# Expert weights of a mixture-of-experts block: loads of 8 KB per partition in 11 of 19 ring places

## The chip, the cores and the metric

The kernel runs on one core of a Trainium2 chip. The metric is device time in microseconds, from launch to the last result, of one execution; the median of three runs is given. Work is spread over five engines: TensorE (PE, with its weight loads shown as PEld), VectorE (DVE), ScalarE (ACT), GpSimd (POOL) and SyncE (SP, which here only issues DMAs). Data come from HBM through 16 DMA engines.

## The reference, cut to what matters

Two transformer blocks are computed on 256 tokens of width 1024, in float32. The first ends with a routed mixture of experts: each token picks one of 4 groups and 2 of its 8 experts, and each of the 32 experts is a gated product with three weight matrices.

```python
def expert_block(args):            # 32 experts, w1 and w3: 1024 x 512, w2: 512 x 1024
    xb, e = args
    hid = jax.nn.silu(xb @ w1[e]) * (xb @ w3[e])
    return hid @ w2[e]
...
x = x + ga1[:, None, :] * (merged @ w_o[l])          # just ahead of it
h2 = modulate(rms_norm(x, g_norm2[l]), sh2, sc2)
x = x + ga2[:, None, :] * hierarchical_moe(h2, ...)  # then the second block
```

All weights of all 32 experts are read: 32 x 6 MB, some 201 MB of the 333 MB that the kernel moves.

## The kernel before, in words

**Stages.** The first block's dense part (modulation, projections, attention, a short convolution) runs until about 215 us, the product with `w_o` and the router until 250 us, the experts until about 720 us, and the second block until 1146 us. In the dense parts each weight tile of 8 KB per partition (`raw`, 7 buffers) is cut by `split_w` (L169) into a rounded part `hi`, written by ACT (L174), and a rest `lo`, written by DVE (L175), each 4 KB per partition with 4 buffers; `mm3` (L188 to L190) then multiplies three times.

**Experts.** They go in 8 groups of four (`QUAD`). Each expert takes at most 32 tokens, so four experts fill the 128 columns of the array side by side. `moe_up` (L1147 on) walks the 1024 rows of `w1` and then of `w3` in 8 blocks of 128 rows each, `moe_down` (L1199 on) the 512 rows of `w2` in 4 blocks. `gather` (L1070 on) picks and turns the tokens of a group: its matmuls (L1079) load columns of `x1` as weights, every second column (`pair`, L471), because a partition holds two neighbouring rows of the expert weights and the tokens' features must come in the same order. The transposes that feed the router (L874) and the modulation's columns (L509) go by the same order.

**The ring.** `plan_experts` lists 192 items of 1 MB: each is two loads of 512 KB, of two experts, with two neighbouring rows of an expert (4 KB without a break) per partition. `fetch_experts` (L1024 on) issues them on SP's queue in this order, into 19 ring places whose buffers are borrowed from other pools: 4 places of kind `w` (two work tiles), 7 of kind `r` (one `raw` tile), 4 of kind `s` (a `hi` and a `lo` tile), 4 of kind `w`. `expert_tiles` takes two items (four loads, one for each expert) out of the queue for each step of two blocks of rows, and asks for the next items behind them. A load waits on SP until PE has read what its buffer held. The last group's `w2` comes in halves of 512 columns (2 KB pieces), in 8 items, so that the second block can begin while the other half is still multiplied.

**Ahead of the experts.** `moving` (L218 on) multiplies by `w_o`; for the second tile of 128 tokens each half of 512 columns is done in two pieces of 256 neighbouring columns. For each piece `fin` adds the residual (L865, L866), sums squares (L917), turns the result (L874) and copies it on POOL (L880); the last piece ends in the router's chain. `fetch_experts(4)` is called before `w_o`'s product, `fetch_experts(RING)` at the start of `moe`.

Of the kernel before, what the change touches and what calls it, by code (L numbers as in the profile page):

```python
# [17 lines left out]
P = 128  # L18
# [65 lines left out]
class Kernel:  # L84
# [133 lines left out]
    def moving(self, W, c0, xT, nk, consume, split=(), halves=False):  # L218
# [6 lines left out]
        for k0 in range(0, nk, 4):  # L225
# [5 lines left out]
            for i, s in order:  # L231
                t, a, b = pieces[i]
                if last:
                    hi, lo = parts[s // 2]
                elif i == 0:
                    hi, lo = split.pop(0) if v is None else self.split_w(v[:, s:s + 2, :])
                for j in range(2):
                    k = k0 + s + j
                    xh, xl = xT(k)
                    self.mm3(ps[i], (xh[:, t * P:(t + 1) * P], xl[:, t * P:(t + 1) * P]),  # L240
                             (hi[:, j, a:b], lo[:, j, a:b]), k == 0, k == nk - 1)
                if last and s == 2:
                    consume(t, ps[i], *([a] if halves else []))
                if (s == 2) if last else (i == len(pieces) - 1):
                    yield
# [172 lines left out]
    def consts_next(self):  # L418
# [19 lines left out]
        self.vec3 = self.half("vec3")[0:12, 0:256]  # L438
        nc.gpsimd.dma_start(self.vec3[0:8], A["b_ada"][:, 3072:5120].rearrange("a (k d) -> (a k) d", d=256))
        nc.gpsimd.dma_start(self.vec3[8:12], A["g_norm2"].rearrange("a (k d) -> (a k) d", d=256))  # L440
        for w, c0, c1 in (("w_rg", 0, 4), ("w_re", 4, 36)):
            for j in range(2):
                nc.sync.dma_start(self.wrt[:, j::2, c0:c1], A[w][0].rearrange("(a p j) c -> p a j c", a=4, j=2)[:, :, j])
# [7 lines left out]
    def consts_late(self):  # L451
# [5 lines left out]
        for j in range(2):  # L457
            nc.tensor.transpose(ps[:, 12 * j:12 * j + 12], self.vec3[:, j::2], self.c("ident")[:12, :12])
        self.cols["vec3"] = c3 = self.const.tile([P, 24], F32, name="vec3c")
        nc.vector.tensor_copy(c3.rearrange("p (r j) -> p r j", j=2), ps[:, 0:24].rearrange("p (j r) -> p r j", j=2))  # L460
# [42 lines left out]
    def ada_cols(self, j, row, cols):  # L503
# [3 lines left out]
        for m in range(4):  # L507
            d = slice(m * P, (m + 1) * P) if j < 4 else self.pair(m)
            nc.tensor.matmul(ps[:, m:m + 1], row[:, d], self.c("every32"), start=True, stop=True)  # L509
# [257 lines left out]
    def block1(self):  # L767
# [91 lines left out]
        for h in range(2):  # L859
            def fin(t, ps, c0):  # L860
                n = ps.shape[1]
                s = slice(h * 512 + c0, h * 512 + c0 + n)
                x1 = self.x1[t]
                tmp = self.half("res")[:, 0:n]
                nc.vector.tensor_tensor(out=tmp, in0=ps, in1=ga1[:, s], op=OP.mult)  # L865
                nc.vector.tensor_tensor(out=x1[:, s], in0=self.xres[t][:, s], in1=tmp, op=OP.add)  # L866
                self.square_piece(t, x1[:, s])
                last = s.stop == D and t == 1
# [4 lines left out]
                for j in range(0, n, P):  # L873
                    turn = nc.tensor.transpose(ps[:, j:j + P], x1[:, self.pair((s.start + j) // P)], self.c("ident"))  # L874
                to, ps = x1T[t][:, s.start // P:s.stop // P], ps.rearrange("p (j t) -> p j t", t=P)
                if t and s.stop < D:
# [3 lines left out]
                nc.gpsimd.tensor_copy(self.xres[t][:, s], x1[:, s])  # L880
# [4 lines left out]
            self.run_all(self.moving(A["w_o"][0], 512 * h, mT, 8, fin, halves=True))  # L885
# [27 lines left out]
    def square_piece(self, t, x):  # L913

        s = self.small([P, 1], "sqp", 6)
        sq = self.half("sq")[:, 0:x.shape[1]]
# [107 lines left out]
    def fetch_experts(self, n):  # L1024

        while len(self.expert_q) < n and self.expert_next < len(self.expert_order):
# [12 lines left out]
            for v, src in zip(to, parts):  # L1039
                self.nc.sync.dma_start(v if len(src.shape) == 2 else v.rearrange("p (j c) -> p j c", j=src.shape[1]), src)  # L1040
            self.expert_q.append(to)

    def expert_tiles(self):

        v = []
        for _ in range(QUAD // 2):
            v += self.expert_q.pop(0)
# [3 lines left out]
    def plan_experts(self):  # L1051


        A = self.A
        self.expert_q, self.expert_order, self.expert_next = [], [], 0
        self.ahead_of = {}
        for e in range(0, NE, QUAD):
            rows = [(A[n], slice(r, r + 256)) for n in ("w1", "w3") for r in range(0, D, 256)]
            if e + QUAD < NE:
                rows += [(A["w2"], slice(r, r + P)) for r in range(0, 512, P)]  # L1060
            for W, r in rows:
                src = [W[0][e + i, r].rearrange("(p j) c -> p (j c)", p=P) for i in range(QUAD)]
                self.expert_order += [src[i:i + 2] for i in range(0, QUAD, 2)]
        for s in range(2):
            for r in range(0, 512, 256):
                src = [A["w2"][0][NE - QUAD + i, r:r + 256, 512 * s:512 * s + 512].rearrange("(j p) c -> p j c", p=P)
                       for i in range(QUAD)]
                self.expert_order += [src[i:i + 2] for i in range(0, QUAD, 2)]

    def gather(self, E, X):  # L1070
# [76 lines left out]
    def moe_up(self, X, late, steps):  # L1147
# [4 lines left out]
        for m in range(2):  # L1152
# [3 lines left out]
            for k0 in range(0, 8, 2):  # L1156
                next(steps, None)
                v = self.expert_tiles()
                for j in range(2):
                    k = k0 + j  # L1160
                    for i in range(QUAD):
                        s = slice(CAP * i, CAP * i + CAP)
                        nc.tensor.matmul(ps[s], X[:, k, s], v[i][:, j * 512:j * 512 + 512], start=k == 0, stop=k == 7,  # L1163
                                         tile_position=(0, CAP * i))
                if late and m == 0 and k0 == 0:
# [7 lines left out]
    def moe_hidden(self, hid):  # L1173
        nc = self.nc
        ps = self.at()
        for f in range(4):
            nc.tensor.transpose(ps[:, f * P:(f + 1) * P], hid[:, f * P:(f + 1) * P], self.c("ident"))
# [21 lines left out]
    def moe_down(self, hid, ET, ws):  # L1199
        hT = self.moe_hidden(hid)  # L1200
        py = [self.mm() for _ in range(2)]
        for f in range(4):
            v = self.expert_tiles()
            for s in range(2):
                self.moe_product(py[s], hT, f, lambda i: v[i][:, s * 512:s * 512 + 512], f == 0, f == 3)
# [7 lines left out]
    def moe_down_last(self, hid, ET, ws):  # L1213
# [4 lines left out]
        for s in range(2):  # L1218
            for f0 in (0, 2):
                v = self.expert_tiles()  # L1220
                for j in range(2):
                    f = f0 + j
                    self.moe_product(py[s], hT, f, lambda i: v[i][:, j * 512:j * 512 + 512], f == 0, f == 3)
# [34 lines left out]
    def overflow_expert(self, e):  # L1258
# [4 lines left out]
        def piece(W, k, c0, twos):  # L1263
            v = self.half("ov_w")
            if twos:
                src = W[bass.ds(e, 1), k // 2 * 256:k // 2 * 256 + 256, c0:c0 + 512]
                src = src.rearrange("a (p j) c -> p (a j) c", j=2)[:, k % 2]
# [488 lines left out]
```

## Time and profile before

| | before |
|---|---|
| runs, median (lowest to highest) | 1146.39 us (1146.24 to 1149.61) |
| the profiled execution's own time | 1147.72 us |
| its span, first to last instruction | 1146.1 us |
| PE busy, share of the span | 91% |
| DVE, ACT busy | 45%, 33% |
| granted TensorE clock, mean | 0.981 |
| moved by DMA | 332.60 MB, 290 GB/s over the span |

The busy shares are averages over stages with different limits, and a busy PE is no measure of its load, since the ends of matmuls are modelled. How to read the stages: the page cuts the span in 40 slices and gives the busy tenths of each engine, the granted clock, the busy share of the DMA engines and the bytes moved; the chain of work that ended last says, followed back, what each piece of work waited for. A row with a line number names the line of the kernel; `out<-in` are its tiles.

### The profile page before, as it was taken

How to read it: one execution, taken by the hardware profiler on the slowest of the kernel's cores; microseconds unless marked ns; L12 is line 12 of the kernel's file. 1: busy time of each engine (PE TensorE's matmuls, PEld its weight loads, DVE VectorE, ACT ScalarE, POOL GpSimd, SP SyncE). 2: the span in 40 equal slices, each digit the busy share in tenths (PEclk: the TensorE clock that was granted, in tenths of full speed). 3: DMA queues.
4: the chain of work that ended last, by engine and by line, in shares of the span. 5: the costliest groups of instructions: out<-in, count | busy, mean ns of one | idle time of the engine just before them, and what ended most of it. 6: DMA issues, size and time to landing. Idle time of an engine off the chain costs nothing.

```text
span 1146.1 us, 16888 instructions
## 1 busy us (share of the span) xinstructions
PE 1047.4 (91%) x6864; PEld 702.1 (61%) x6866; DVE 515.4 (45%) x882; ACT 383.5 (33%) x618; POOL 47.8 (4%) x60
## 2 busy tenths in 40 slices
PE   5999999989978888888888888999899999999998
PEld 2787699964231313131212213977889899999987
DVE  3776565651130211212121203797577765555555
ACT  3443444521010100000000003766547564444454
POOL 1030000000000000000000000222110000000000
PEclk9999999989989999999999999999999999999999
DMA  9798887889999999999999999955333655555521
GB/s 343 272 365 281 300 280 265 289 324 407 409 409 408 409 408 409 409 409 408 409 410 409 409 404 375 316 159 155 118 102 121 212 190 184 184 184 184 166 74 37
DMA packets 148035, 332.60 MB, mean 290 GB/s; under 512 B 11717, under 2 KB 61729, under 8 KB 147953
## 3 DMA queue, kind: packets, MB, share of 16 engines
q1 hardware_dynamic: 146624, 328.95, 78.2%
q0 software_dynamic: 688, 1.38, 0.4%
q8 instruction: 55, 0.90, 0.3%
q10 hardware_dynamic: 640, 1.14, 0.3%
q14 instruction: 28, 0.22, 0.0%
HBM read 330.38 MB, written 1.05 MB: 289 GB/s over the span
## 4 chain that ended last, share of the span: by engine, by line
PE 54%; DMA 38%; DVE 5%; ACT 2%; issue 1%; SPq 0%; DVEq 0%; ACTq 0%
DMA ew<-w 15%; DMA raw<-w 14%; PE mm L188 13%; PE mm L189 13%; PE mm L190 13%; DMA lo<-w 7%; PE pa L496 2%; DVE lo L175 1%; PE pa L623 1%; DMA raw<-w_ada 1%; PE pb L189 1%; PE pa L189 1%; PE pb L190 1%; PE pa L190 1%; PE pa L188 1%
## 5 line engine op out<-in xcount | busy, mean ns | idle before, releaser
L175 DVE TENSOR_TENSOR lo<-raw,hi 128x1024 fp32r<-128x1024 f32 x192 | 235.3, 1229 | 124.8 <-ACT hi L174 124.1
L174 ACT ACTIVATE hi<-raw 128x1024 fp32r<-128x1024 f32 x192 | 201.8, 1058 | 180.3 <-PE mm L189 109.0
L1163 PE MATMUL mm<-ew,moeX 128*32 128x512 f32 x432 | 112.7, 602 | 14.6 <-DMA ew<-w 14.6
L188 PE MATMUL mm<-hTh,hi 128*128 128x256 f32 x416 | 120.8, 290 | 0.0
L190 PE MATMUL mm<-hTh,lo 128*128 128x256 f32 x416 | 119.3, 287 | 0.0
L189 PE MATMUL mm<-hTl,hi 128*128 128x256 f32 x416 | 118.8, 286 | 0.0
L1170 DVE TENSOR_TENSOR hid<-hid,mm 128x512 f32<-128x512 f32 x8 | 5.5, 687 | 225.3 <-PE mm L1163 225.3
L1163 PE MATMUL mm<-raw,moeX 128*32 128x512 f32 x376 | 92.0, 610 | 11.8 <-DMA raw<-w 10.5
L189 PE MATMUL mm<-fTl,hi 128*128 128x256 f32 x352 | 99.7, 283 | 0.0
L188 PE MATMUL mm<-fTh,hi 128*128 128x256 f32 x352 | 99.6, 283 | 0.0
L190 PE MATMUL mm<-fTh,lo 128*128 128x256 f32 x352 | 99.6, 283 | 0.0
L188 PEld LDWEIGHTS mm<-hTh,hi 128*128 128x128 f32 x416 | 80.1, 192 | 5.6 <-issue 2.4
L190 PEld LDWEIGHTS mm<-hTh,lo 128*128 128x128 f32 x416 | 80.1, 193 | 1.8 <-issue 1.4
L189 PEld LDWEIGHTS mm<-hTl,hi 128*128 128x128 f32 x416 | 80.1, 193 | 1.2 <-issue 1.0
L1163 PEld LDWEIGHTS mm<-ew,moeX 128*32 128x32 f32 x432 | 20.2, 108 | 96.3 <-DMA ew<-w 77.6
L188 PEld LDWEIGHTS mm<-fTh,hi 128*128 128x128 f32 x352 | 67.5, 192 | 0.5
L189 PEld LDWEIGHTS mm<-fTl,hi 128*128 128x128 f32 x352 | 67.5, 192 | 0.4
L190 PEld LDWEIGHTS mm<-fTh,lo 128*128 128x128 f32 x352 | 67.5, 192 | 0.0
L1163 PEld LDWEIGHTS mm<-raw,moeX 128*32 128x32 f32 x376 | 17.0, 109 | 77.1 <-DMA raw<-w 56.9
L1195 DVE SCALAR_TENSOR_TENSOR y<-mm,moews,ga 128x512 f32<-128x512 f32 x16 | 12.0, 748 | 92.9 <-PE mm L1186 92.9
L1140 ACT ACTIVATE moeET<-pb 128x256 fp32r<-128x256 f32 x8 | 3.1, 383 | 148.1 <-PE pb L1138 148.1
L188 PE MATMUL mm<-hi,hTh 128*128 128x512 f32 x128 | 51.9, 407 | 0.0
(405 smaller groups left out, 1843.3 us busy)
## 6 DMA issues: line engine op xcount, KB each, us to landing
ew<-w SPq DMA_DIRECT2D x164, 512.0 KB, 10.2
raw<-w SPq DMA_DIRECT2D x140, 512.0 KB, 10.2
raw<-w_in SPq DMA_DIRECT2D x42, 1024.0 KB, 9.5
raw<-w_ada SPq DMA_DIRECT2D x24, 1024.0 KB, 11.7
hi<-w SPq DMA_DIRECT2D x40, 512.0 KB, 10.2
lo<-w SPq DMA_DIRECT2D x40, 512.0 KB, 10.2
raw<-w_ffn_gate SPq DMA_DIRECT2D x11, 1024.0 KB, 5.3
raw<-w_ffn_up SPq DMA_DIRECT2D x11, 1024.0 KB, 5.4
```

What stands on the lines that cost most here:

```text
L174: nc.scalar.activation(out=hi, in_=v, func=AF.Copy)
L175: nc.vector.tensor_tensor(out=lo, in0=v, in1=hi.bitcast(F32), op=OP.subtract)
L188: nc.tensor.matmul(out, lh, rh, start=first, stop=False, **kw)
L189: nc.tensor.matmul(out, lh, rl, start=False, stop=False, **kw)
L190: nc.tensor.matmul(out, ll, rh, start=False, stop=last, **kw)
L496: nc.tensor.matmul(ps[32 * g:32 * g + 32], self.cb[:, 4 * half + g, :], v[half][:, g, :], start=half == 0, stop=half == 1, tile_position=( ...
L623: nc.tensor.matmul(o, qz[h // 4][:, h % 4, t * P:(t + 1) * P], key(h)[:, 0:L], start=True, stop=True)
L1140: nc.scalar.activation(out=ET, in_=ps[:, 0:T], func=AF.Copy)
L1163: nc.tensor.matmul(ps[s], X[:, k, s], v[i][:, j * 512:j * 512 + 512], start=k == 0, stop=k == 7, tile_position=(0, CAP * i))
L1170: nc.vector.tensor_tensor(out=hid, in0=hid, in1=up[1], op=OP.mult)
L1195: self.nc.vector.scalar_tensor_tensor(out=y, in0=ps, scalar=ws, in1=self.ga2[:, sl], op0=OP.mult, op1=OP.mult)
```

## The change

An item of the ring becomes four neighbouring rows of one expert (8 KB without a break per partition, 1 MB in all) instead of two rows of two experts. In places of kind `r` and `s` (11 of 19) it is one load of 1 MB; in places of kind `w`, whose two work tiles are separate, it stays two loads with 4 KB per partition each, the front and the back half of each 8 KB piece. For that, `hi` and `lo` of `split_w` become the two halves of one tile of 8 KB per partition (tag `spl`, 4 buffers). A step takes four items instead of two and works on four blocks of rows. Two places of the order stay fine (two items a step, two experts an item): the first four items of all, and the last four of `w3` in the last group; the last group's `w2` stays in 2 KB pieces. The features now come in fours: `gather`, the transposes for the router and the modulation's columns read every fourth column, and for the second tile of tokens `moving` takes, as a piece of 256 columns, two neighbours of every four instead of 256 neighbours, so that `fin` works on such columns too. The router's weights and some vectors are loaded in the same order.

```diff
 def split_w(self, v):
-        hi = self.spl_p.tile([P, a, b], F32R, tag="hi", name="hi")
-        lo = self.spl_p.tile([P, a, b], F32R, tag="lo", name="lo")
+        both = self.spl_p.tile([P, 2, 1024], F32R, tag="spl", name="hilo")
+        hi, lo = (both[:, i, 0:a * b].rearrange("p (a b) -> p a b", a=a) for i in range(2))
...
 def moving(...):
+                    o, w = ps[i], [x[:, j, a:b] for x in (hi, lo)]
+                    if fours and t:
+                        o, w = o.rearrange("p (g f) -> p g f", f=2), [self.fours(x[:, j], a // 128) for x in (hi, lo)]
...
-    def pair(k):
-        o = 256 * (k // 2) + k % 2
-        return slice(o, o + 255, 2)
+    def every(n, k):
+        o = n * P * (k // n) + k % n
+        return slice(o, o + n * (P - 1) + 1, n)
+    def fours(a, c):
+        return a.rearrange("p (g f) -> p g f", f=4)[:, :, c:c + 2]
...
 def fetch_experts(self, n):
-            if kind == "r":
-                r = self.raw()
-                to = [r[:, 0:1024], r[:, 1024:2048]]
-            elif kind == "s":
-                to = [self.spl_p.tile([P, 1024], F32, tag=tag, name=tag) for tag in ("hi", "lo")]
+            if kind == "w":
+                to = [self.work("ew") for _ in range(2)]
             else:
-                to = [self.work("ew") for _ in range(2)]
+                t = self.raw() if kind == "r" else self.spl_p.tile([P, 2048], F32, tag="spl", name="es")
+                to = [t[:, 0:1024], t[:, 1024:2048]]
+            if len(parts) == 1 and kind != "w":
+                self.nc.sync.dma_start(t, parts[0])
+            else:
+                if len(parts) == 1:
+                    parts = [parts[0][:, 0:1024], parts[0][:, 1024:2048]]
...
 def plan_experts(self):
-            rows = [(A[n], slice(r, r + 256)) for n in ("w1", "w3") for r in range(0, D, 256)]
+            rows = [(A[n], slice(r, r + 512)) for n in ("w1", "w3") for r in range(0, D, 512)]
...
-                self.expert_order += [src[i:i + 2] for i in range(0, QUAD, 2)]
+                if (e, n) in ((0, 0), (NE - QUAD, 3)):
+                    for h in range(2):
+                        half = [a[:, 1024 * h:1024 * h + 1024] for a in src]
+                        self.expert_order += [half[i:i + 2] for i in range(0, QUAD, 2)]
+                        self.expert_fine.append(True)
+                else:
+                    self.expert_order += [[a] for a in src]
+                    self.expert_fine.append(False)
...
 def gather(self, E, X):
-                    nc.tensor.matmul(o[j], self.x1[t][:, self.pair(k0 + j)], E[:, t], start=t == 0, stop=t == 1)
+                    nc.tensor.matmul(o[j], self.x1[t][:, self.every(4, k0 + j)], E[:, t], start=t == 0, stop=t == 1)
```

## Rows read from the trace of the kernel before

**Rows 1.** Page, part 4: the chain that ended last, shares by engine.
```profile
PE 54%; DMA 38%; DVE 5%; ACT 2%; issue 1%; SPq 0%; DVEq 0%; ACTq 0%
```

**Rows 2.** The chain in order of time: start us, us, what.
```profile
254.13 1.85 PE mm L1163 x16
...
262.37 10.29 DMA raw<-w
...
683.96 10.79 DMA ew<-w
694.79 1.92 PE mm L1186 x10
```

**Rows 3.** Windows: length, busy us of engines (count), clock, DMA share, GB/s.
```profile
149.00:156.00 7.00, 7.00 (x61) 7.00 (x60) 2.92 (x4) 2.18 (x3) 0.00 (x0) 1.00 1.10 348
686.00:704.00 18.00, 13.54 (x62) 5.12 (x64) 7.08 (x14) 6.41 (x13) 0.00 (x0) 0.91 1.05 387
300.00:650.00 350.00, 295.51 (x1382) 88.57 (x1379) 54.43 (x120) 26.74 (x53) 0.00 (x0) 0.97 1.03 409
```

**Rows 4.** DMA view of the same three windows, in that order: packets by size.
```profile
DMA packets 2405, 2.44 MB, mean 348 GB/s; under 512 B 39, under 2 KB 2389, under 8 KB 2405
...
DMA packets 3594, 6.96 MB, mean 387 GB/s; under 512 B 195, under 2 KB 195, under 8 KB 3594
...
DMA packets 39253, 143.15 MB, mean 409 GB/s; under 512 B 4355, under 2 KB 4355, under 8 KB 39233
```

**Rows 5.** Page, part 6: loads into raw by SP, KB each, us to landing.
```profile
raw<-w SPq DMA_DIRECT2D x140, 512.0 KB, 10.2
```

**Rows 6.** SP's queue, waits: two rows of 262:700 us, then one of 246:262.
```profile
SPq L1040 <- DMA ew<-w: 120.8, 133, 2.4
...
SPq L1040 <- PE mm L1163: 2.3, 6, 1.0
...
SPq L1040 <- PE mm L1163: 10.9, 3, 8.6
```

**Rows 7.** Timeline of SP's queue, 254.5:264 us: start, us, loads issued.
```profile
255.99 4.98 SPq L1040 DMA_DIRECT2D ew<-w  x8
```

**Rows 8.** Windows at the experts' start, and three of 10 us inside.
```profile
254.00:258.00 4.00, 4.00 (x38) 1.79 (x40) 0.82 (x2) 0.85 (x2) 0.00 (x0) 1.00 0.45 145
...
310.00:320.00 10.00, 7.14 (x31) 2.98 (x29) 2.15 (x7) 0.38 (x1) 0.00 (x0) 0.93 1.03 411
340.00:350.00 10.00, 6.88 (x27) 1.76 (x31) 1.87 (x4) 0.00 (x0) 0.00 (x0) 0.54 1.03 408
350.00:360.00 10.00, 9.15 (x54) 1.91 (x50) 0.00 (x0) 0.60 (x1) 0.00 (x0) 1.00 1.02 407
```

**Rows 9.** One line's instructions, L874 and L313: duration ns min/median/max.
```profile
L874 PEld LDWEIGHTS pb<-cst,x x16: 194/209/221, 225.8 to 243.4; 128*128 128x128 f32 x16
...
L313 PEld LDWEIGHTS pb<-cst,xres x48: 138/140/230, 700.2 to 1120.7; 128*128 128x128 f32 x48
```

**Rows 10.** The chain again: runs of matmuls with such weights.
```profile
255.98 1.14 PE pb L1079 x8
...
716.31 0.96 PE pb L313 x7
```

**Rows 11.** Timeline of PE in the product with w_o: two neighbouring matmuls.
```profile
224.38 0.28 PE L190 MATMUL mm<-hi,ml 128*128 128x256 f32 x1
224.50 0.28 PE L188 MATMUL mm<-hi,mh 128*128 128x256 f32 x1
```

**Rows 12.** Groups by line and shape, 224:262 us: DVE and ACT on one piece.
```profile
L866 DVE TENSOR_TENSOR x<-xres,res 128x256 f32<-128x256 f32 x4 | 1.9, 468 | 0.1
...
L917 ACT ACTIVATE sq<-x 128x256 f32<-128x256 f32 x4 | 1.7, 415 | 2.7 <-DVE x L866 2.7
```

**Rows 13.** Page, part 5: the split's first half on ACT.
```profile
L174 ACT ACTIVATE hi<-raw 128x1024 fp32r<-128x1024 f32 x192 | 201.8, 1058 | 180.3 <-PE mm L189 109.0
```

**Rows 14.** Page, part 3: the queue with the largest packets.
```profile
q8 instruction: 55, 0.90, 0.3%
```

More of the change, by code (lines that the diff above doesn't have):

```diff
@@ L216, in stat_unit, with moving @@
             yield
-    def moving(self, W, c0, xT, nk, consume, split=(), halves=False):
+    def moving(self, W, c0, xT, nk, consume, split=(), halves=False, fours=False):
         split = list(split)
@@ L437, in consts_next @@
             ("norm_ffn_g_2", 8), ("norm_ple_g_2", 8))], nc.gpsimd)
-        self.vec3 = self.half("vec3")[0:12, 0:256]
-        nc.gpsimd.dma_start(self.vec3[0:8], A["b_ada"][:, 3072:5120].rearrange("a (k d) -> (a k) d", d=256))
-        nc.gpsimd.dma_start(self.vec3[8:12], A["g_norm2"].rearrange("a (k d) -> (a k) d", d=256))
+        self.vec3 = self.half("vec3")[0:6]
+        nc.gpsimd.dma_start(self.vec3[0:4], A["b_ada"][:, 3072:5120].rearrange("a (k d) -> (a k) d", d=512))
+        nc.gpsimd.dma_start(self.vec3[4:6], A["g_norm2"].rearrange("a (k d) -> (a k) d", d=512))
         for w, c0, c1 in (("w_rg", 0, 4), ("w_re", 4, 36)):
-            for j in range(2):
-                nc.sync.dma_start(self.wrt[:, j::2, c0:c1], A[w][0].rearrange("(a p j) c -> p a j c", a=4, j=2)[:, :, j])
+            for a in range(2):
+                nc.sync.dma_start(self.wrt[:, 4 * a:4 * a + 4, c0:c1],
+                                  A[w][0][512 * a:512 * a + 512].rearrange("(p j) c -> p j c", j=4))
         spread(self.brt[:, 0:4], "b_rg", 4)
@@ L860, in fin @@
             def fin(t, ps, c0):
-                n = ps.shape[1]
-                s = slice(h * 512 + c0, h * 512 + c0 + n)
+                n, k0 = ps.shape[1], 4 * h + c0
+                cut = (lambda a: self.fours(a, c0)) if t else (lambda a: a)
+                part = lambda a: cut(a[:, h * 512:h * 512 + 512])
+                flat = (lambda a: a.rearrange("p (g f) -> p g f", f=2)) if t else (lambda a: a)
                 x1 = self.x1[t]
[L864 to L868, printed above, removed]
+                tmp = flat(self.half("res")[:, 0:n])
+                nc.vector.tensor_tensor(out=tmp, in0=flat(ps), in1=part(ga1), op=OP.mult)
+                nc.vector.tensor_tensor(out=part(x1), in0=part(self.xres[t]), in1=tmp, op=OP.add)
+                self.square_piece(t, part(x1), flat)
+                last = k0 == 6
                 if last:
@@ L873, in fin @@
                 for j in range(0, n, P):
-                    turn = nc.tensor.transpose(ps[:, j:j + P], x1[:, self.pair((s.start + j) // P)], self.c("ident"))
-                to, ps = x1T[t][:, s.start // P:s.stop // P], ps.rearrange("p (j t) -> p j t", t=P)
-                if t and s.stop < D:
+                    turn = nc.tensor.transpose(ps[:, j:j + P], x1[:, self.every(4, k0 + j // P)], self.c("ident"))
+                to, ps = x1T[t][:, k0:k0 + n // P], ps.rearrange("p (j t) -> p j t", t=P)
+                if t and not last:
                     nc.scalar.activation(out=to, in_=ps, func=AF.Copy)
@@ L884, in fin @@
                     self.router(1, mean, self.router_logits(x1T[1], range(6, 8), logits, turn))
-            self.run_all(self.moving(A["w_o"][0], 512 * h, mT, 8, fin, halves=True))
+            self.run_all(self.moving(A["w_o"][0], 512 * h, mT, 8, fin, halves=True, fours=True))
         for t in range(2):
@@ L1155, in moe_up @@
                 next(steps, None)
[L1156 to L1165, printed above, removed]
+            v = []
+            for k in range(8):
+                if k % 2 == 0:
+                    next(steps, None)
+                if not v:
+                    v = self.expert_tiles()
+                for i in range(QUAD):
+                    s = slice(CAP * i, CAP * i + CAP)
+                    nc.tensor.matmul(ps[s], X[:, k, s], v[i].pop(0), start=k == 0, stop=k == 7,
+                                     tile_position=(0, CAP * i))
+                v = v if v[0] else None
+                if late and m == 0 and k == 1:
                     late()
@@ L1176, in moe_hidden @@
         for f in range(4):
-            nc.tensor.transpose(ps[:, f * P:(f + 1) * P], hid[:, f * P:(f + 1) * P], self.c("ident"))
+            nc.tensor.transpose(ps[:, f * P:(f + 1) * P], hid[:, self.every(2, f)], self.c("ident"))
         hT = self.half("hidT")
```

55 lines of the change are left out of this document (31 added, 24 removed).

## The prediction, made before the changed kernel was run

> **What bounds the kernel now.** I read the chain of work that ended last first. By engine it is 54% PE and 38% DMA [rows 1], which sounds like a mixture; followed in time it is two stages with one bound each. Up to 254 us and from 695 us on it runs through PE, DVE and ACT; from 262 to 695 us it is nothing but expert loads, one landing after the other, each piece some 10 us long [rows 2]. So 432 us are bound by the DMA engines, and what PE does there costs nothing as long as it keeps up. The windows say how close that stretch is to a limit: 409 GB/s at a DMA share of 1.03 over 350 us [rows 3]. Nothing is idle there, so only the engines' own rate can shorten it. The waits of SP's queue agree: in this stretch it waits for earlier loads (120.8 us for one kind alone), and hardly for PE to give a buffer back (2.3 us) [rows 6]. A load lands 10.2 us after its issue [rows 5], which at 409 GB/s is eight loads of 512 KB, so only 4 of the ring's 19 MB are under way at a time, and the ring has slack.
>
> **What a packet costs.** Three stretches with a DMA share over 1, each with one packet size, tell what the size is worth [rows 3, 4]. Without the small packets below 512 B, 149 to 156 us has 1 KB packets, 686 to 704 us has 2 KB (6.96 MB over 3,399) and 300 to 650 us has 4 KB (143 MB over some 34,900). The time of one packet on one of 16 engines is 16 times its size over the rate: 16 x 1024 / 348 = 47.1 ns, 16 x 2048 / 387 = 84.7 ns, 16 x 4096 / 409 = 160.2 ns. The steps are 37.6 ns for the first KB added and 75.5 ns for the next two (37.8 each): a straight line, 37.7 ns per KB and some 9.4 ns per packet whatever its size. The share of completion packets (one behind eight of 4 KB) is inside the 160.2, and stays one behind eight in a 1 MB load with 8 KB packets.
>
> **The gain.** On that line an 8 KB packet takes 160.2 + 2 x 75.5 = 311.2 ns, two of 4 KB take 320.4. A 1 MB item is 8 such packets on each engine, so it saves 8 x 9.2 = 74 ns of 2.56 us, 2.9%. The number of such items in the DMA-bound stretch comes from the plan. Of 192 items, 0 to 3 and 180 to 191 stay fine. The first 19 are issued ahead of the experts, where SP is held by others; item 19 is the first that waits for PE's first step (issued at 255.99 us [rows 7]). From 19 to 179, places 4 to 14 of the ring occur 8 x 11 = 88 times in the full rounds (items 19 to 170), and 5 times in the last (175 to 179): 93. Gain: 93 x 0.074 = 6.8 us. Ends of the unknown: nothing, if the hardware cuts an 8 KB piece back into 4 KB packets; and, if a packet cost nothing beyond its bytes, 93 x 8 x 18.8 ns = 14.0 us. Between them I take the line, which three points support; rounding of the rates moves it by 0.3 us.
>
> The items in places of kind w stay 4 KB packets, but from rows 8 KB apart. The 2 KB packets of 686 to 704 us are halves of 4 KB rows, too, and lie on the line, so 0. Twice the bytes per load doubles what eight loads hold in flight to at most 8 MB, still within the ring, 0. Some hundred issues on SP fall away; it was waiting anyway.
>
> The Trainium skill has a figure that speaks against this size of gain. On the page "DMA: Bandwidth & Descriptors", section "Why small descriptors are slow (HBM only)", it gives a fixed overhead of some 3 cycles per packet; 32 bytes go in a cycle, so 4 KB takes 131 cycles and 8 KB 259 instead of 262, 1.1%, and the sum would be 2.7 us instead of 6.8. The trace disagrees: its 9.4 ns are 5.9% of a 4 KB packet.
>
> **PE in the experts' stretch.** A step now waits for four items instead of two and then does four blocks of rows. Two blocks take 1.85 us at full clock (the 16 instructions of [rows 2]), four 3.7 us, while four items take some 10.1 us to land. PE works in bursts now, and the clock may fall: before, 340 to 350 us was granted 0.54, nearly the lower level of 1.2 GHz, in a stretch with idle times of PE, and 350 to 360 us, where PE worked on with hardly a gap, 1.00 [rows 8]. At 1.2 GHz throughout, the four blocks take 7.4 us, still under 10.1; and a PE that falls behind works without gaps, which is when the full clock is granted. The remaining slack is the ring, 15 items or some 37 us behind the group in use. Cost 0; if that cover were gone the wait would show on SP for PE. The end of the stretch keeps its fine steps, so what follows the last landing is unchanged.
>
> **The start of the stretch.** Here PE's path counts in full: the DMA engines run dry (share 0.45 from 254 to 258 us [rows 8]), because SP waited up to 8.6 us for PE's first step [rows 6]. The first four items stay fine, so the first eight loads are issued as before, 10.3 us of work from 255.99 us [rows 2, 7]. The third and fourth step become one, so the first `raw` buffer comes back some 2 us later, near 264 us; the queue then still holds some 2 us. Cost 0.
>
> **What lies on PE's path ahead of it.** (a) Weight loads that read every fourth column: 32 for the modulation's columns, 16 transposes (L874), 32 of the first `gather`, 80 in all. No row has this step. Every second column instead of neighbours made the load itself 209 ns instead of 140 [rows 9], while the matmuls with such weights still follow each other by 1.14/8 = 0.143 us against 0.96/7 = 0.137 [rows 10]: hidden behind the matmul. Bounds 0 and 80 x 0.069 = 5.5 us; I take 0.5, nearer the row of the spacing. (b) 96 matmuls of `w_o` (2 pieces, 8 blocks, 3 products, 2 halves) whose moving operand is two neighbours of every four. They follow each other by 0.12 us [rows 11]. No row has such an operand; bounds 0 and a doubling, 96 x 0.12 = 11.5 us. I take 0. (c) DVE and ACT on such columns: on the last piece two of DVE (0.47 us) and one of ACT (0.42) lie on the path [rows 12]; bounds 0 and a doubling, 1.3 us; I take 0.3. POOL's copy has the whole first group to finish. (d) `hi` and `lo` in one tile: ACT now waits for the last of the three products instead of the second, 0.12 us later [rows 13, 11], with three further buffers filled; 0.
>
> On (a) and (b) the Trainium skill, page "SBUF — State Buffer", in its note on cachelines under the port swizzle, says that two accesses in each 16-byte line run at full bandwidth and fewer pay. By it (b) is free and (a) pays; that the load with every second column, which has two, took 209 ns instead of 140 is not what that rule says, and the sum keeps the bounds of rows.
>
> **The sum.** -6.8 + 0.5 + 0.3 = -6.0 us. The profiled execution took 1147.72 us (span 1146.1, so 1.6 around it), 1.3 above the median of the three runs; 1147.72 - 6.0 = 1141.7, and against the median 1146.39 it is 1140.4. What comes next behind the faster stream is still the stream.
>
> **The rivals.** First, 8 KB pieces travel as 4 KB packets: no gain, and the 0.8 us of the start remain, 1147.2. For it speaks that no packet of SP's loads here is above 4 KB, since none was asked for; against it, that the instruction queue has 55 packets of 16 KB [rows 14], so the engines take larger ones. The skill's page on DMA, section "SWDGE vs HWDGE vs iDMA", prefers packets of at most 4096 B, which would make this the outcome; no run shows whether it holds for SP's queue.
> Second, the per-packet cost is smaller than the line's: a gain of 2.7, 1144.5 with the costs; the line speaks against.
> Third, on the other side: pairs out of four as moving operand run at half rate in the product with `w_o`. All of its 11.5 us lie ahead of PE's first step, where SP waits for PE, so they come in full: 1140.4 + 11.5 = 1151.9. It decides once (b) passes 6 us, a slowdown by half. For it speaks (a)'s 209 against 140 ns; against it, that spacing did not follow.
> Fourth, 8 KB packets run slower than two of 4 KB. The 16 KB packets took 0.3% x 16 x 1146 / 55 = 1.0 us each [rows 14], where four of 4 KB take 0.64; but they come one by one, to another place, with their latency inside. Even a tenth of that excess, (1.0 - 0.64) / 2 x 0.1 = 18 ns for 8 KB, would be 93 x 8 x 18 ns = 13 us and 1159.
>
> **How the numbers follow.** The line 0.64, no gain 0.16, the small gain 0.06, half-rate `w_o` 0.10, slow 8 KB packets 0.04. The forecast is the likeliest, 1140.4. Its own range: costs at most some 2.6 us above what I took (1143.0), and a gain a third of the way from 6.8 to 14.0 with no cost (1146.4 - 9.2 = 1137.2). To leave out no more than 2 in 10 the range reaches over the small gain and no gain, to 1148. A measurement of this kernel tells a change of 0.3%, 3.4 us, from none: below 1142.95 is faster. That is the forecast's 0.64, less 0.02 for its upper tail, 0.62; the same is 0.02 + 0.16 + 0.06 = 0.24; slower 0.14.
>
> **What would show it.** Right: over the middle of the experts' stretch some 416 GB/s instead of 409 (11/19 of the bytes 2.9% faster), packets of 8 KB in the DMA view and some 29% fewer packets of data for the same bytes (half as many for 11/19 of them); the last expert load landing some 6 us earlier; the stretch from 695 us on moved as a block. Wrong in the gain: 409 GB/s and no packet of 8 KB. Wrong at the start: PE's first expert step later than 254.1 us, with L188 to L190 of the w_o product further apart than 0.12 us, or L1079 further than 0.143. Wrong on PE: SP waiting for PE inside the stretch for more than a few us, or DMA shares below 1 there.

## The result, and the profile after

| | before | after |
|---|---|---|
| median of 6 runs (lowest to highest) | 1147.30 us (1146.24 to 1149.61) | 1154.62 us (1152.60 to 1155.78) |
| the profiled execution's own time, its span | 1147.72, 1146.1 us | 1154.68, 1153.1 us |

The ratio of after to before is 1.0058 (95% interval 1.0046 to 1.0070): the changed kernel is slower by 7.3 us, where 6 us less was forecast, and lies 6.6 us above the end of the range.

The chain of work that ended last (start us, us, what) divides it into three, as [rows 2] did before:

```profile
270.86 2.65 PE mm L1192 x16
...
695.63 10.77 DMA ew<-w
706.45 1.92 PE mm L1216 x10
```

| stage | before | after | difference |
|---|---|---|---|
| up to the first expert step | 254.13 us | 270.86 us | +16.7 |
| from there to the last landing | 440.7 us | 435.6 us | -5.1 |
| from there to the end of the span | 451.3 us | 446.7 us | -4.6 |

**The stream** did what was forecast. The window of its middle (columns as in [rows 3]) and the DMA view of it answer to [rows 3, 4]:

```profile
300.00:650.00 350.00, 260.94 (x1453) 105.22 (x1454) 57.35 (x126) 27.36 (x54) 0.00 (x0) 0.88 1.02 416
```
```profile
DMA packets 28073, 145.58 MB, mean 416 GB/s; under 512 B 3116, under 2 KB 3116, under 8 KB 17516
```

The rate is 416 GB/s instead of 409. Without the small packets there are 24,957 packets where there were 34,898, which is 28% fewer, and 10,557 of them (28,073 less 17,516) are of 8 KB or more. The granted clock fell from 0.97 to 0.88, at a DMA share that stayed above 1.

**The start** did not. First, two neighbouring matmuls of the product with `w_o` (timeline of PE; start us, duration), for [rows 11]:

```profile
223.83 0.41 PE L188 MATMUL mm<-hilo,mh 128*128 128x256 f32 x1
224.06 0.41 PE L189 MATMUL mm<-hilo,mh 128*128 128x256 f32 x1
```

They are 0.23 us apart instead of 0.12. Second, the chain's runs of matmuls whose weights are every fourth column: a set of modulation columns (L517; the chain of before has L509 x8 with 0.83 us), and a run of `gather` behind the first step, for the 1.14 us of [rows 10]:

```profile
116.38 1.75 PE pb L517 x8
...
273.51 2.06 PE pb L1107 x8
```

The instructions of these lines (duration ns min/median/max) say that the load of weights is what grew, but not for the transposes:

```profile
L1107 PEld LDWEIGHTS pa<-moeEr,x x8: 330/330/330, 268.6 to 270.2; 128*128 128x128 f32 x8
```
```profile
L884 PEld LDWEIGHTS pb<-cst,x x16: 196/206/261, 235.8 to 259.6; 128*128 128x128 f32 x16
```

In `gather` a load takes 330 ns (197 at the median for those into `pa` before), in the transposes 206, as in [rows 9] with every second column. Third, two stretches at half the clock (1.2 GHz of 2.4), each beginning within a microsecond of the end of a set of modulation columns; before was granted 1.00 from 100 to 150 us throughout:

```profile
119.00:122.00 3.00, 3.00 (x12) 2.27 (x12) 0.80 (x3) 1.95 (x3) 0.00 (x0) 0.50 0.49 184
...
137.00:139.00 2.00, 2.00 (x11) 1.88 (x10) 0.86 (x2) 0.67 (x2) 0.00 (x0) 0.50 1.02 353
```

### The profile page after: what moved, and what is told of

Read it like the earlier page. It is cut to its first block, busy times and chain, and to the rows that moved or that the text cites. A ratio compares the mean times of both kernels' runs of the same rounds, so it can differ in the third digit from the quotient of the medians.

```text
span 1153.1 us, 16719 instructions
## 1 busy us (share of the span) xinstructions
PE 1018.3 (88%) x6866; PEld 732.6 (64%) x6868; DVE 515.3 (45%) x882; ACT 383.4 (33%) x618; POOL 48.2 (4%) x60
## 3 DMA queue, kind: packets, MB, share of 16 engines
q10 hardware_dynamic: 640, 1.14, 0.3%
## 4 chain that ended last, share of the span: by engine, by line
PE 59%; DMA 33%; DVE 5%; ACT 2%; issue 1%; SPq 0%; DVEq 0%; ACTq 0%
DMA ew<-w 16%; PE mm L188 13%; PE mm L190 13%; PE mm L189 13%; DMA raw<-w 10%; DMA es<-w 6%; PE pa L504 2%; PE mm L1216 2%; PE mm L1192 2%; PE pa L631 1%; PE pb L1107 1%; DVE hilo L175 1%; PE pa L1107 1%; DMA raw<-w_ada 1%; PE pb L517 1%
## 5 line engine op out<-in xcount | busy, mean ns | idle before, releaser
L175 DVE TENSOR_TENSOR hilo<-raw,hilo 128x1024 fp32r<-128x1024 f32 x192 | 235.3, 1229 | 131.9 <-ACT hilo L174 131.5
L174 ACT ACTIVATE hilo<-raw 128x1024 fp32r<-128x1024 f32 x192 | 201.8, 1057 | 165.1 <-PE mm L190 107.5
L188 PE MATMUL mm<-hTh,hilo 128*128 128x256 f32 x416 | 120.6, 290 | 0.0
L190 PE MATMUL mm<-hTh,hilo 128*128 128x256 f32 x416 | 119.2, 287 | 0.0
L189 PE MATMUL mm<-hTl,hilo 128*128 128x256 f32 x416 | 118.6, 285 | 0.0
L189 PE MATMUL mm<-fTl,hilo 128*128 128x256 f32 x352 | 99.6, 283 | 0.0
L190 PE MATMUL mm<-fTh,hilo 128*128 128x256 f32 x352 | 99.5, 283 | 0.0
L188 PE MATMUL mm<-fTh,hilo 128*128 128x256 f32 x352 | 99.5, 283 | 0.0
L188 PEld LDWEIGHTS mm<-hTh,hilo 128*128 128x128 f32 x416 | 80.1, 193 | 5.8 <-issue 2.5
L190 PEld LDWEIGHTS mm<-hTh,hilo 128*128 128x128 f32 x416 | 80.1, 193 | 1.9 <-issue 1.5
L189 PEld LDWEIGHTS mm<-hTl,hilo 128*128 128x128 f32 x416 | 80.1, 193 | 1.2 <-issue 1.0
L188 PEld LDWEIGHTS mm<-fTh,hilo 128*128 128x128 f32 x352 | 67.4, 192 | 0.5
L190 PEld LDWEIGHTS mm<-fTh,hilo 128*128 128x128 f32 x352 | 67.5, 192 | 0.0
L188 PE MATMUL mm<-hilo,hTh 128*128 128x512 f32 x128 | 51.5, 404 | 0.0
L189 PE MATMUL mm<-hilo,hTh 128*128 128x512 f32 x128 | 50.7, 396 | 1.0 <-DVE hilo L175 1.0
```

Source lines behind the costliest of these rows:

```text
L188: nc.tensor.matmul(out, lh, rh, start=first, stop=False, **kw)
L189: nc.tensor.matmul(out, lh, rl, start=False, stop=False, **kw)
L190: nc.tensor.matmul(out, ll, rh, start=False, stop=last, **kw)
```

## The experiments

The theory after the result: PE's strided reads ahead of the first step cost the 16.7 us (S). The rival: PE in bursts, at the lower clock of 0.88, costs it, by the coarse steps (B). All times below are medians, with the ratio to the kernel before. That kernel's median was 1147.30 us beside the changed kernel and 1147.73 to 1147.99 us beside the others, so differences between kernels are good to some 0.7 us. The times in a chain come from one execution of each kernel.

### The strided reads, one at a time

**The moving operand alone.** The halves of `w_o` are written by ACT and DVE in another order of columns, so that PE reads 256 neighbours; for the first tile of tokens DVE's multiplication puts the columns back. All else is the changed kernel.

```diff
+    def split_w4(self, v):
+        src = v.rearrange("p j c -> p (j c)").rearrange("p (m c f) -> p c m f", c=2, f=2)
+        hi, lo = (both[:, i].rearrange("p (c m f) -> p c m f", c=2, f=2) for i in range(2))
...
-                        o, w = o.rearrange("p (g f) -> p g f", f=2), [self.fours(x[:, j], a // 128) for x in (hi, lo)]
+                        w = [x[:, a // 256, j] for x in (hi, lo)]
...
```

> The changed kernel with one part undone: in the product with w_o the split writes hi and lo already in the order in which the pieces need them, so that PE reads 256 neighbouring columns again (it read two of every four). Theory S (PE reads such pairs at half rate, and all of that lies ahead of the experts): the matmuls of the second tile of tokens follow each other by 0.12 us instead of 0.23, 96 x 0.11 = 10.6 us come back, 1144 us, first expert step near 260 us instead of 270.9. Theory B (the loss comes from PE working in bursts of four blocks, with its clock at 0.88 in the experts' stretch instead of 0.97): nothing comes back, 1154 us.

Measured: 1143.57 us, ratio 0.9962 (0.9950 to 0.9974), 11.05 less than the changed kernel. In its chain the first expert step begins 11.65 us earlier:

```profile
259.21 2.93 PE mm L1211 x16
```

**The weight loads alone.** The modulation rows and the tokens are stored in fours, by the copies and additions that write them anyway, so that PE loads 128 neighbours, in the router's transposes too.

```diff
-        nc.vector.tensor_copy(row, ps)
+            nc.vector.tensor_copy(row.rearrange("p (f g) -> p f g", f=4), ps.rearrange("p (g f) -> p f g", f=4))
...
-                nc.vector.tensor_tensor(out=part(x1), in0=part(self.xres[t]), in1=tmp, op=OP.add)
+                nc.vector.tensor_tensor(out=x1n, in0=nat(part(self.xres[t])), in1=nat(tmp), op=OP.add)
...
-                    nc.tensor.matmul(o[j], self.x1[t][:, self.every(4, k0 + j)], E[:, t], start=t == 0, stop=t == 1)
+                    nc.tensor.matmul(o[j], self.x1[t][:, (k0 + j) * P:(k0 + j + 1) * P], E[:, t], start=t == 0, stop=t == 1)
```

> The changed kernel with the other strided reads undone: the modulation's rows and x1 are stored with their features already in fours, so that the weight loads of the modulation's columns, of the router's transposes and of gather read neighbouring columns; the pairs in the product with w_o stay. Theory S: eight loads of columns take 0.83 us again instead of 1.75, four times 0.92 = 3.7 us, the first gather gives some 2 us back and the half clock near 120 us goes (1.7): 7 us in all, 1147.5 us, eight of gather's matmuls in 1.14 us instead of 1.87 to 2.06. Theory B: within 1 us of 1154.6.

Measured: 1148.78 us, ratio 1.0011 (1.0001 to 1.0020), 5.84 less than the changed kernel. A set of modulation columns takes 0.79 us, there is no stretch at half the clock from 100 to 150 us, and the first step comes 6.58 us earlier:

```profile
115.97 0.79 PE pb L520 x8
...
264.28 2.53 PE mm L1197 x16
```

**Both.**

> Both of the above together: 8 KB packets and coarse steps as in the changed kernel, but PE reads no strided columns. Theory S: 1154.6 - 10.6 - 7 = 1137, that is some 9 to 10 us below the kernel before (6.8 of packets, the rest what differs in the second block), first expert step near 254 us, 416 GB/s in the experts' stretch with PE's clock still below 0.95 there. Theory B: no better than the kernel before, 1147 or more.

Measured: 1139.97 us (1138.60 to 1141.25), ratio 0.9929 (0.9916 to 0.9943), 14.65 less than the changed kernel and faster than the kernel before. The clock in the middle of the stream is still 0.89, so B is out as the cause of the loss. But the two parts don't add up: alone they moved the first step by 11.65 and 6.58 us, together by 13.95 (to 256.91), 4.3 less than the sum. The groups by line show one reason: the repair costs DVE something, which PE's slow product had hidden. The addition on 256 columns, 426 ns in the changed kernel, takes 1004 ns in the mean when it writes in fours (two of the four 1.3 to 1.4 us, two 0.6 us):

```profile
L900 DVE TENSOR_TENSOR x<-xres,res 128x256 f32<-128x256 f32 x4 | 4.0, 1004 | 0.1
```

**Both, with POOL turning the tokens.** The addition goes back to the natural order, and the copy that POOL makes in any case writes the tokens in fours; the router's transposes read every fourth column again.

```diff
-                nc.gpsimd.tensor_copy(part(self.xres[t]), part(x1))
+                nc.gpsimd.tensor_copy(x1f, fine(part(x1)))
```

> The kernel with both reads made contiguous (1139.97 us), with one difference: the residual is added in place in the natural order of columns, the router's transposes read every fourth column again, and POOL's copy, not DVE's addition, writes the tokens in fours for the gather. If the price of the repair lies in DVE's addition (its row grew from 426 to 1004 ns for 256 columns, and 1.3 us of it stand in the chain behind each of the two last pieces), the first expert step begins 1.3 to 2.6 us earlier than 256.9, and the time is 1137.4 to 1138.7 us. If the two repairs overlap for another reason, or if the gather now waits for POOL's copy, the first step stays at 256.9 or comes later and the time is 1140 or more.

Measured: 1139.31 us (1138.11 to 1139.66), ratio 0.9924 (0.9910 to 0.9938). The first step comes 2.46 us earlier than the 256.91 of the version above, and is again where the kernel before had it (254.13):

```profile
254.45 2.71 PE mm L1216 x16
...
679.24 10.78 DMA ew<-w
690.06 1.92 PE mm L1240 x10
```

The medians are only 0.7 us apart, less than expected, and the runs of the two overlap: the worth of this last step in the whole time is not settled.

With it the start adds up, if each chain is cut at the first of the four sets of columns that the change strides and at the first matmul of the product with `w_o` (start in us, then the length of the two parts):

| kernel | first set | `w_o` | first expert step | set to `w_o` | `w_o` to step |
|---|---|---|---|---|---|
| before | 104.76 | 215.76 | 254.13 | 111.00 | 38.37 |
| no strided reads, POOL turning | 104.50 | 215.34 | 254.45 | 110.84 | 39.11 |
| no strided reads, DVE turning | 105.51 | 216.35 | 256.91 | 110.84 | 40.56 |
| strided loads alone | 105.50 | 220.22 | 259.21 | 114.72 | 38.99 |
| strided `w_o` alone | 104.45 | 215.30 | 264.28 | 110.85 | 48.98 |
| the changed kernel | 103.89 | 221.77 | 270.86 | 117.88 | 49.09 |

The strided `w_o` costs 9.9 us (39.11 to 48.98), the strided loads 3.9 (110.84 to 114.72), the turning on DVE 1.45 (39.11 to 40.56), which is within what was expected; the other 1.0 us of the 2.46 lie ahead of `w_o`, where these two versions are the same program. The changed kernel has another 3.2 us ahead of `w_o` (114.72 to 117.88), and its two stretches at half the clock lie there. The version with strided loads alone runs the same program up to `w_o` and has none, so they vary from one execution to the next. Of the kernels whose columns are loaded with every fourth, two of three profiled executions have one or two such stretches; of the eight others none has. What sets them off is not shown. Both repairs came out without them, so that these 3.2 us were counted twice; with the 1.7 that DVE's turning took back from the gain behind `w_o`, and 0.5 the other way ahead of the first set, that is the 4.3.

### The operand by itself

32 matmuls of each kind, each with 128 x 128 weights, behind the kernel before; the added work lengthens the span to 1232.9 us. The granted clock is 1.00 in all of it.

```diff
+        for _ in range(n):
+            nc.tensor.matmul(o, w, m[:, 256:512], start=True, stop=True)
+        for _ in range(n):
+            nc.tensor.matmul(o, w, m[:, 0:512:2], start=True, stop=True)
+        for _ in range(n):
+            nc.tensor.matmul(two(o, 2), w, four[:, :, 0:2], start=True, stop=True)
+        for _ in range(n):
+            nc.tensor.matmul(two(o, 4), w, eight[:, :, 0:4], start=True, stop=True)
...
+            nc.tensor.matmul(q, f[:, 0:256:2], f[:, 512:640], start=True, stop=True)
...
```

> The kernel before with blocks of 32 equal matmuls behind its end, to measure PE's reads by themselves: float32r matmuls of 256 columns whose moving operand is contiguous, every second, two of four, four of eight, eight of sixteen, every fourth; then float32 matmuls of 128 columns whose weights are contiguous, every second, every fourth, every eighth column. Theory S by 16-byte pieces: the cost follows how much of each 16 bytes is used: contiguous, four of eight and eight of sixteen 0.12 us each, every second and two of four 0.23, every fourth 0.23 or more; weights 0.14 us per matmul for contiguous and every second column, 0.25 for every fourth. Rival (any step costs the same): four of eight and eight of sixteen at 0.23 too, and weights in every second column slower than contiguous.

The chain of its end, moving operands of 256 columns in the split type first (contiguous; every second; two of every four; four of eight; eight of sixteen; every fourth), then float32 weights (contiguous; every second; every fourth; every eighth), where a matmul is two instructions:

```profile
1153.59 3.84 PE mm L1753 x32
1157.42 7.25 PE mm L1755 x32
1164.68 7.25 PE mm L1757 x32
1171.93 3.77 PE mm L1759 x32
1175.70 3.84 PE mm L1761 x32
1179.54 7.46 PE mm L1763 x32
1187.00 7.15 PE mm L1766 x64
1194.15 7.54 PE mm L1768 x64
1201.69 14.93 PE mm L1770 x64
1216.62 15.22 PE mm L1772 x64
```

Per instruction: a moving operand costs 0.120 us contiguous, 0.227 with two of every four, and 0.118 with four of every eight. Weights cost 0.112 contiguous, 0.118 with every second column and 0.233 with every fourth. So both new reads of the change are of the kind that halves PE's rate, and the read that the kernel before had, every second column as weights, is not.

### The packets

**The changed kernel, every item in two loads of 4 KB per partition.** Strides, tiles and steps stay.

```diff
-            if len(parts) == 1 and kind != "w":
+            if False:
```

> The changed kernel with every expert item in two loads of 4 KB per partition (front and back half of the 8 KB piece), order and steps unchanged: the packet size alone undone. Theory of the packet's fixed cost (9.4 ns): the stretch goes back to 409 GB/s and 93 x 0.074 = 6.8 us are added, 1161 us. Rival (the stream did not gain by packet size but by the order of rows or fewer issues): 416 GB/s and 1154.6 us stay.

Measured: 1160.55 us, ratio 1.0105 (1.0089 to 1.0120), 5.9 us more than the changed kernel. The middle of the stream is back at the rate of [rows 3], at the clock of after:

```profile
300.00:650.00 350.00, 258.49 (x1440) 102.10 (x1441) 56.71 (x124) 26.35 (x53) 0.00 (x0) 0.88 1.03 409
```

**The same without the strided reads.**

> The version without strided reads, with every expert item in two loads of 4 KB per partition: coarse steps and the order in fours remain, 8 KB packets do not. Packet theory: 1140.0 + 93 x 0.074 = 1146.9, 409 GB/s. What then remains against the kernel before is what the coarse steps, the start and the second block cost or give together, near 0 to -1. Rival (coarse steps with their low clock cost several us that the packets hide): 1149 or more.

Measured: 1146.15 us, ratio 0.9991 (0.9982 to 1.0000), 6.2 us more than with 8 KB pieces (1139.97). The chains say the same of the stage alone: from the first step to the last landing 441.7 us in 4 KB pieces (first two lines), 435.4 in 8 KB pieces (last two), 6.3 less.

```profile
255.59 1.85 PE mm L1216 x16
...
697.26 1.92 PE mm L1240 x10
```
```profile
256.91 2.49 PE mm L1216 x16
...
692.30 1.92 PE mm L1240 x10
```

**More places of one load.** The contiguous kernel, with the 8 places of kind `w` used in the first round only.

```diff
-            kind = RING_KINDS[self.expert_next % RING]
+            i = self.expert_next
+            kind = RING_KINDS[i] if i < RING else RING_KINDS[4 + (i - RING) % (RAW + SPL)]
```

> The version without strided reads, with the places of two work tiles used in the first round of the ring only; from item 19 on all items go to the 11 places that take 8 KB without a break. Packet theory: items 19 to 179 are all 8 KB, 161 instead of 93, 68 x 0.074 = 5.0 us less, 1135, 422 GB/s in the stretch. Rival (a ring of 11 MB is too short for PE's bursts and pauses at the end of a group): SP waits for PE inside the stretch, DMA share under 1, 1140 or more.

Measured: 1142.74 us, ratio 0.9955 (0.9941 to 0.9970), 2.8 us more than with the 19 places, although the stream runs faster. Two windows, the DMA view of the second, and SP's waits in 270:680 us:

```profile
260.00:264.00 4.00, 4.00 (x38) 2.02 (x40) 0.83 (x3) 0.46 (x1) 0.00 (x0) 1.00 0.00 0
...
300.00:650.00 350.00, 248.98 (x1416) 85.28 (x1412) 54.42 (x120) 27.34 (x54) 0.00 (x0) 0.90 1.01 421
```
```profile
DMA packets 20223, 147.37 MB, mean 421 GB/s; under 512 B 2247, under 2 KB 2247, under 8 KB 2247
```
```profile
SPq L1073 <- PE mm L1217: 129.7, 39, 9.7
```

421 GB/s is 1.2% over 416, over some 390 us of stream an estimated 4.6 us. But with 11 places the next loads wait for PE to finish steps of four items, and the DMA engines stand still at the start: share 0.00 from 260 to 264 us, 0.01 in the next four, where the kernel with 19 places had 0.80 and 0.92, and some 7 us are gone.

### The merged tile

The kernel before, with `hi` and `lo` in one tile of 8 KB and nothing else; places of kind `s` take the new tile.

```diff
-        hi = self.spl_p.tile([P, a, b], F32R, tag="hi", name="hi")
-        lo = self.spl_p.tile([P, a, b], F32R, tag="lo", name="lo")
+        both = self.spl_p.tile([P, 2, 1024], F32R, tag="spl", name="hilo")
+        hi, lo = (both[:, i, 0:a * b].rearrange("p (a b) -> p a b", a=a) for i in range(2))
...
-                to = [self.spl_p.tile([P, 1024], F32, tag=tag, name=tag) for tag in ("hi", "lo")]
+                r = self.spl_p.tile([P, 2048], F32, tag="spl", name="es")
+                to = [r[:, 0:1024], r[:, 1024:2048]]
```

> The kernel before with one part of the change alone: hi and lo as the two halves of one tile; items, steps and order of columns as before. Theory N (the merged tile changes nothing but who waits for whom by 0.1 us): 1147.7, within 1 us. Theory T: the second block is 4 to 5 us shorter in all kernels with the merged tile (from the first matmul behind the last expert load to the end 451.3 us before, 446.7 after), so the merged tile is where that comes from: 1143 to 1144, with the idle time of 3.0 us that PE shows near 803 us gone.

Measured: 1144.30 us, ratio 0.9973 (0.9964 to 0.9981), 3.7 us less than the 1147.99 of the kernel before. The last landing is at 695.85 us, 1.1 later than before; the gain lies behind it, where 451.3 us became 447.7. Most of it is in one place of the second block, ahead of a run of small matmuls. First the kernel before, its chain and two windows, then this kernel, its chain and one window:

```profile
802.95 2.96 issue
```
```profile
806.00:809.00 3.00, 3.00 (x57) 2.96 (x58) 1.43 (x5) 0.00 (x0) 1.28 (x2) 0.61 0.91 339
809.00:812.00 3.00, 3.00 (x23) 3.00 (x23) 1.26 (x5) 0.97 (x2) 0.00 (x0) 0.82 0.00 0
```
```profile
803.68 1.14 issue
```
```profile
807.00:810.00 3.00, 3.00 (x28) 3.00 (x27) 1.73 (x7) 1.39 (x3) 1.07 (x2) 1.00 0.80 302
```

PE is idle for 1.14 us instead of 2.96 without waiting for anything that the profile shows, and the granted clock doesn't fall to 0.61 behind the gap. That is 1.8 us, and some 1.5 for the 16 matmuls that follow each other by 0.21 us instead of 0.12. The kernel of the matmul blocks, which still has two tiles, shows the gap again, with 2.69 us. What shortened it was not tried: fewer waits on PE's queue, since two tiles became one, is an argument and no more. Of the 4.6 us by which the changed kernel is faster behind the last landing, 1.0 is not accounted for.

## Why the prediction was wrong, point by point

Four steps lead from before to after, and the medians give each step's price; the second step bundles several parts:

| step | forecast | measured |
|---|---|---|
| merged tile (1147.99 to 1144.30) | 0 | -3.7 us |
| fours, coarse steps, no strided read, 4 KB pieces (to 1146.15) | +0.3 | +1.9 us |
| 8 KB pieces (to 1139.97) | -6.8 | -6.2 us |
| strided reads (to 1154.62) | +0.5 | +14.7 us |

The prices are good to some 0.7 us, as said above. The second step holds the price of the turning on DVE, too: 40.48 us from `w_o` to the first step, where POOL's turning has 39.11. That is 1.4 of the 1.9, and what is left for the fours and the coarse steps, 0.5, is within the error.

**What bounds the kernel, and the packets: right.** The straight line in the packet size held. In the version with more places all 17,976 packets of data in the window (20,223 less 2,247 small ones) are of 8 KB; 16 x 8192 / 421 GB/s is 311.3 ns, and the line gave 311.2. The rate of 416 GB/s and the packets' count were as listed under what would show it. The gain is 6.2 us by the one pair of medians, 5.9 by the other, and 6.3 by the stage: near the 6.8. The chain of before was read a little too simply: it leaves the loads once, for 5.1 us near 400 us, in a stretch whose rate does not change. The two rivals without a full gain and the one of slow 8 KB packets fell with this. By the Trainium skill's 3 cycles per packet ("DMA: Bandwidth & Descriptors", "Why small descriptors are slow (HBM only)") the gain from 4 to 8 KB would have been an estimated 1.1%; between 409 and 421 GB/s it is 2.9%.

**(b), the moving operand: wrong, and the largest error.** It was taken at 0 of 0 to 11.5 us. It measured 9.9 us between `w_o` and the first step and 11.05 in the time (the version with a contiguous `w_o` had no half clock, which may be a part of this); 96 matmuls by 0.11 us, the difference of the spacings, are 10.6. This was the third rival, which had a chance of 0.10 and a time of 1151.9 us. The step that failed is the choice within the bounds. No row had such an operand; what spoke for 0 was the spacing of matmuls whose *weights* were strided [rows 10], and that is another read with another tolerance. By the Trainium skill ("SBUF — State Buffer", "Door 1: The DMA port swizzle", the note on cachelines) two accesses in each line of 16 bytes run at full bandwidth, and pairs out of four would be free; the probe's 0.227 us against 0.120 speaks against that for a moving operand, while four of every eight, which fill whole lines of 16 bytes, took 0.118.

**(a), the weight loads: wrong.** It was taken at 0.5 of 0 to 5.5. It measured 3.9 us ahead of `w_o`, and 5.84 in the time together with the half clock. The four sets of modulation columns took 1.75 us each instead of 0.79, 4 x 0.96 = 3.8 us; the 16 loads of `gather` ahead of the first step, in the changed kernel, 4.08 us where before had 3.49, 0.6 more. Two readings failed. The 209 ns of [rows 9] belong to transposes, and transposes stayed at 206 with every fourth column; the gather's own loads, 197 ns with every second, went to 330. And "hidden behind the matmul" was true of a load of 197 ns only: with 330 ns the instructions follow each other by 2.06/8 = 0.26 us instead of 0.14. For weights the same note of the Trainium skill held: every second column, two accesses in a line, cost 0.118 against 0.112, and every fourth 0.233. I had the rule in the text and let the wrong row outvote it. One strided read of the change stood in no list: the transposes of the hidden rows (L1207) now load every second column, 208 ns instead of 142, but they lie inside the stream.

**The clock: half right.** In the stream it fell to 0.88, and cost nothing, as argued: the DMA share stays at 1.02. But on PE's path two drops appeared that no part of the sum had, and in the profiled execution 3.2 us with them. That a PE without gaps gets the full clock, as [rows 8] had been read, did not hold there: PE was busy for 3.00 of 3 us at 0.50.

**The start: the term was mis-sized.** The cost of the coarse steps was taken as 0, with 2 us of queue to spare. Four kernels in the 16 us behind their first step, at 254 us or, the last, at 255.59: before, the merged tile alone, POOL turning the tokens, and the version without strided reads in 4 KB pieces:

```profile
254.00:270.00 16.00, 16.00 (x146) 5.89 (x144) 1.63 (x5) 1.97 (x4) 0.00 (x0) 1.00 0.88 342
```
```profile
254.00:270.00 16.00, 16.00 (x133) 5.82 (x136) 1.63 (x5) 1.97 (x4) 0.00 (x0) 0.92 0.80 307
```
```profile
254.00:270.00 16.00, 16.00 (x135) 5.82 (x137) 1.63 (x5) 1.97 (x4) 0.00 (x0) 0.93 0.77 283
```
```profile
255.59:271.59 16.00, 16.00 (x145) 5.72 (x144) 1.63 (x5) 1.97 (x4) 0.00 (x0) 1.00 0.83 307
```

At 409 GB/s the 59 GB/s that the third lacks over 16 us are 2.3 us. The fourth, with coarse steps at the full clock, lacks 35 GB/s, 1.4 us, and its stage from the first step to the last landing is 441.7 us long where before had 440.7: 1.0 to 1.4 us go with the coarse steps. SP waited there up to 9.9 us for a step of PE, in the third up to 12.1, where [rows 6] had 8.6. The merged tile alone lacks 35 GB/s, too, without coarse steps, but at a clock of 0.92: its first 16 matmuls took 3.02 us instead of 1.85. The third has both, and the rest of its 2.3 us, 0.9, goes with its clock of 0.93. Whether the merged tile, which all but before have, has a share is not shown. In the changed kernel, too, the first 16 took 2.65 us, so that both stand between the gain by the packets and the stream's -5.1 us.

**(c): right**, in that DVE and ACT with columns two by two cost nothing that shows: 426 ns for the addition where [rows 12] had 468. **(d), the merged tile: wrong by 3.7 us**, a gain in a stage that the prediction had moved as a block. The listed sign of an error at the start, a first step later than 254.1 us with L188 to L190 further apart than 0.12, was the one that appeared.

## What to carry to other kernels

A new layout of the data in memory is paid by whoever reads it with a stride: before such a change, list every operand of TensorE that it turns from contiguous to strided, moving and weights apart, and look for a row of exactly that kind. Where there is none, and the path counts in full, a block of 32 such matmuls behind the kernel settles it. The cure here was to let the engine that writes the operand do the turning, and then to see whether that engine had come onto the path.

## What the runs showed of the hardware

- A moving operand of 256 columns of the split type runs at half rate with every second column (0.227 us against 0.120) and with two of every four (0.227), hardly slower with every fourth (0.233), and at full rate with four of every eight (0.118).
- Float32 weights are nearly free with every second column (0.118 us an instruction against 0.112), double with every fourth (0.233), and not worse with every eighth (0.238). A transpose's load takes 140 ns contiguous, 209 with every second column and no more with every fourth (206).
- A load with 8 KB without a break per partition travels in packets of 8 KB, and the rates of four stretches with packets of 1, 2, 4 and 8 KB (348, 387, 409 and 421 GB/s) give a packet the same 9.4 ns beside its bytes.
- PE can be idle for 3 us ahead of a run of small matmuls without waiting for anything in the profile, and with two tiles made one 1.8 us of it were gone (2.96 to 1.14).
- The granted clock was 1.2 GHz (0.50) from 119 to 122 us in the changed kernel while PE showed no gap, and 2.4 GHz (1.00) there in a version that is the same program up to that place.
